# Order of steps and the scheduler's seed in a two-layer encoder trunk on one core

## The chip, the cores and the metric

The kernel runs on one core of a Trainium2 chip. The metric is the device time of one execution in microseconds (us). Before the change the median of three runs is 1641.14 us (1639.19 to 1641.91).

The names of the engines are those of the profile: PE is the tensor engine (matmuls; PEld are its weight loads), DVE the vector engine, ACT the scalar engine, POOL is GpSimd and SP the engine that only starts transfers (DMAs).

## The reference

Two layers, each a token sublayer and a channel sublayer, on x of 512 tokens by 1024 channels in float32:

```python
for i in range(DEPTH):
    proj = x @ w_in[i]
    q_na, k_na, v_na, q_r, k_r, v_r, g_r, gate_a, gate_b = jnp.split(proj, IN_SPLITS, axis=-1)
    ya = neighbourhood_attention(...)          # 8 heads of 64, windows of 8 rows x 16 columns
    yb = bidirectional_retention(q_r, k_r, v_r, g_r, ...)  # 4 heads, chunks of 128, rotary
    merged = sigmoid(gate_a) * (ya @ w_branch_a[i]) + sigmoid(gate_b) * (yb @ w_branch_b[i])
    x = layer_norm(ALPHA * x + merged @ w_out[i], ln1_g[i], ln1_b[i])
    ffn = conv_glu_ffn(x, w_up[i], conv_w[i], conv_b[i], w_down[i])     # width 2816, conv of 3 tokens
    ple = sigmoid(x @ w_ple_gate[i]) * (p[i] @ w_ple_proj[i])
    x = layer_norm(ALPHA * x + ffn + ple, ln2_g[i], ln2_b[i])
```

In `bidirectional_retention` q and k are rotated by position, scores between the tokens of a chunk are weighted with a decay, and a state of decayed k times v is carried from chunk to chunk, in both directions.

## The kernel before

**One matmul.** Every float32 operand is split in two: `hi` is its cast to a shorter format (ACT) and `lo` what is left (DVE subtracts). `mm3` (line 1181) makes three matmuls of each product, hi by hi, hi by lo and lo by hi. So each weight tile of 128x1024 (512 KB) comes in by a DMA (tiles `raw`, `rawa`, `rawt`), ACT writes `hi`, DVE writes `lo`, and only then PE can use it. In PE's rows, `u<-sx,lo` writes the accumulator `u` from the operands `sx` and `lo`.

**Seven products in place of eight.** Large products are cut into 2x2 blocks and done with seven products of sums of blocks, called a, c, t1, t2, d, t3, t4. The sums of weights are made in the loading: POOL adds a second weight tile to the first with an accumulating DMA, or, where two tiles are "mates", DVE adds them. The sums of x are made by `vg_sums` (line 1454), a generator that does one of its four steps each time it is called. In a step name the digit is the block, so `0t3` is product t3 of block 0.

**Stages of a layer.** First the v and g stretch (products of blocks 0 and 1, `vg`, line 1491; in layer 2 the gate block 9 too), then the fill stretch: q, k and gate blocks 2 to 8, the retention heads R0 to R3 and the neighbourhood heads N0 to N7. A retention head (`ret_head`, line 1625) takes several turns: PE transposes the rotated k (`kf`) to `kz`, DVE scales `kz`, PE makes scores `s` from `qk`, DVE weights them (`ta`, `a`, with the decay table `wx`), PE makes the state `st` from `kz` and v, DVE copies it to `su`, and PE writes the output `o` from `a`, `su` and `qx`. Then the output projection, the norm (`xn`, transposed by PE as `tr`), the gate of the layer embedding together with the first MLP segment (`pg`), and the other two MLP segments (`up_part`, `down`). `affine` (the steps A0 to A3) is six half-row DVE operations (two multiplications and four additions) that nothing on PE waits for soon; "g" is a plain tile of the up-projection without the seven products.

**What sets the order.** Every instruction is first recorded (`Program`, line 239) and emitted later by `run` (line 272), so all rows of the profile carry line 278. PE keeps the order in which the code asks for the matmuls, except that in the fill stretch it may choose among the next 10 groups (`FILL_WIN`). That order is written in tables: `VG` (v and g), `FILL`, `PG` (embedding gate and first MLP segment), `UP_ORDER` (segments 2 and 3), and `SUMS_AT` (at which steps of the v and g stretch a step of `vg_sums` is taken). ACT, DVE, POOL and SP are ordered by a list scheduler: `_dues` (line 422) gives each instruction a due time from the PE instructions that need it, `_order` (line 563) plays the whole program with modelled durations and picks the ready instruction with the earliest due, and `_best` (line 494) repeats that for 120 rounds with randomly raised due times, and keeps the round with the shortest modelled end. `SEED` starts the random numbers. There are two plans, one for each layer, from early in the v and g stretch to the end of the MLP. What lies outside keeps the order of the code.

**Mates.** `up_items` (line 931) makes the weight tiles of an MLP segment s; its last argument says whether t2 and t3 of a block take DVE's addition (mates) or POOL's.

Of the kernel before, what the change touches and what calls it, by code (L numbers as in the profile page):

```python
# [42 lines left out]
FILL_WIN = 10  # L43
FILL_AT = (36, 40, 56, 24, 28, 8, 20, 52)
FILL = (tuple('2a 7a 2c 7c 7t1 2t1 2t2 7t2 2d 7d 2t3 7t3 7t4 2t4 3a 8a R0 8c R1 3c R0 3t1 8t1 R1 R0 R1 8t2 R0 8d 8t3 3t2 3d 8t4 3t3 4a R1 4c 3t4 5a R2 4t1 5c R2 R3 R3 5t1 4t2 R2 5t2 R3 R2 4d 5d 5t3 4t3 R3 6a 6c 6t1 N0 N1 6t2 5t4 vn 6d N3 N1 6t3 4t4 6t4 vn N0 bb0 N2 vn vn bb2 N2 N0 N5 N2 N1 N3 N4 N6 bb3 bb1 N4 N5 N6 N6 bb4 N7 bb5 N4 N5 xn N3 N7 bb6 N7 bb7'.split()),
        tuple('9t2 X0 2a X1 2c X3 X2 9t3 9d 7a 7c 2t1 9t4 7t1 7t2 7d 2t2 2d 2t3 7t3 2t4 7t4 3a 8a R0 R0 3c 8c 3t1 R1 8t1 R1 R0 R1 8t2 R0 8d 8t3 3t2 3d 4a 8t4 3t3 R1 4c 3t4 5a R2 4t1 5c R2 R3 R3 5t1 4t2 R2 5t2 R3 R2 5d 5t3 4d 4t3 R3 6a 6c 6t1 N0 N1 6t2 5t4 vn 6d N3 N1 6t3 4t4 N0 vn 6t4 vn N2 N3 vn bb0 bb2 N0 N2 N5 N1 N2 N6 N4 N6 bb3 N4 bb1 N7 N5 N6 bb4 N4 bb5 bb7 N3 xn N5 N7 bb6 N7'.split()))
ORD = ('vector', 'scalar', 'tensor', 'gpsimd', 'sync')
BA = (tuple('0 1 2 3 4 5 6 7'.split()),
        tuple('0 1 2 3 4 5 6 7'.split()))
NORM = 'vector'  # L50
MATES = (1, 2)
FILL_MATES = ((), (0, 1))
WO = ('a', 'c', 't1', 't2', 'd', 't3', 't4a', 'T0', 't4b')

VG0 = ('p0', 'p1', '0a', '0c', '1a', '1c', 'ga0', '0t1', 'ga2', 'ga1', '0t2', '0d', '0t3', '1t1', '0t4', 'ga3', '1t2', '1d', '1t3', '1t4')
VG1 = ('0a', '0c', '1a', '1c', '9a', '0t1', '9c', '0t2', '0d', '1t1', '0t3', '0t4', '9t1', '1t2', '1d', '1t3', '1t4')
VG = (VG0, VG1)
SENT = ((20, 24), (24, 32))
CAST = ((32, 36), (44, 52))

TABLES_AT = ('0t4', '1t4')

PG = (tuple('a 0a T2 c S g S 0c S S g 1a t1 t2 0t1 1c 0t2 0d 0t3 1t1 0t4 d g 1t2 1d 1t3 t3 1t4 g t4'.split()),
        tuple('a 0a T2 S c S 0c 1a g g S 1c t1 0t1 S 0t2 t2 0d 0t3 1t1 0t4 1t2 1d 1t3 d 1t4 g t3 g t4'.split()))
PG_EARLY = "a"
A_DEEP = (4, 5, 5)
BOUND = ("p0", "t4a", "tr", "t4b", "p1")
VG_DEEP = 3
VG_PLAN = ("ga2", "0a")
SUMS_AT = (('1c', '0t1', 'ga1', 'ga2'), ('1c', '9a', '0t1', '9c'))  # L70
VG_EARLY = "d"
S_SEQ = ("t1", "d", "t2", "t3")
UP_ORDER = ((tuple('0a 0t1 A0 0c g A2 0t2 A3 A1 0d 0t3 1a 0t4 1t1 1c 1t2 1d 1t3 2a 1t4 2t1 2c 2t2 2d 2t3 s 2t4 s s'.split()), tuple('0a 0t1 0c g 0t2 0d 0t3 1a 0t4 1t1 1c 1t2 1d 1t3 2a 2t1 2t2 2d 2t3 2c 1t4 s 2t4 s s'.split())),
            (tuple('0a 0t1 A0 0c A1 g A2 0t2 A3 0d 0t3 1a 0t4 1t1 1c 1t2 1d 1t3 2a 1t4 2t1 2c 2t2 2d 2t3 s 2t4 s s'.split()), tuple('g 0a 0t1 0c g 0t2 0d 0t3 g 0t4 1a 1t1 1c 1t2 1d 1t3 s g s 1t4 s s'.split())))

DOWN = ("a", "c", "t1", "t2", "d", "t3", "t4")
# [8 lines left out]
SET = {1: dict(soon=5, hold=6, reserve=10, load=16, work=25, scale=1.0, spare=2, near=10, seed=0, shake=0.0), 2: dict(soon=5, hold=6, reserve=10, load=16, work=25, scale=1.0, spare=2, near=10, seed=0, shake=0.0)}  # L85
ROUNDS = 120
WALK = 12
SEED = 1


VG_HELD = (('0t1', '1t1', '0t2', '0c', '1t2', '1a', '1d', '1t3'), ('0a', '0c', '0t1', '1t1', '1t3', '1t2', '0t3', '0t2', '1d'))
# [7 lines left out]
def _up_order(l, s):  # L99

    return UP_ORDER[l][s - 1] if s else PG[l]


def _up_blocks(l, s):

    t0 = 2 * sum(SEGS[:s])
    return [t0 + 2 * b for b in range(sum(k[0].isdigit() and k.endswith("t4") for k in _up_order(l, s)))]
# [386 lines left out]
def _best(jobs, rounds=None):  # L494

    import random
    rnd = random.Random(SEED)
    rounds = rounds or ROUNDS
# [289 lines left out]
def trunk(tc, wpack, x_nat, x_tr, head, p_tr, rpb, decay, ln_par, ln_col, conv, cos_t, sin_t, dist, xi_d, zd, ident_d, out):  # L788
# [5 lines left out]
    with ExitStack() as es:  # L794
# [66 lines left out]
        def block_items(pos, held, early, n=2, mates=False):  # L861

            out = []
            prev = {}
            for kind, src, plus in (("a", "a", None), ("c", "c", None), ("t1", None, "b"), ("t2", None, "d"),
                                    ("d", "d", None), ("t3", "b", "d"), ("t4", None, "c")):
                for j in range(n):
                    at = lambda q: None if q is None else pos[q, j]
                    it = Item(kind, at(src), pos["a", j][3], plus=at(plus), own=kind in ("a", "t3"), pool=held.get(kind))
                    if kind in ("a", "t1", "t2", "t4"):  # L870
                        if j in prev:
                            prev[j].nxt = it
                        prev[j] = it
                    if kind == "t3":
                        [o for o in out if o.kind == early][j].early = it
                    out.append(it)
            if mates:
                t2, d, t3 = ([o for o in out if o.kind == k] for k in ("t2", "d", "t3"))
                for j in range(n):
                    t2[j].mate, t3[j].mate, d[j].then = d[j], d[j], t3[j]  # L880
            return out
# [49 lines left out]
        def up_items(l, s):  # L931

            t0, by = 2 * sum(SEGS[:s]), {}
            for b, t in enumerate(_up_blocks(l, s)):
                pos = {(q, 0): (l, UP0 + 2 * t + i, 0, 1024) for i, q in enumerate("acbd")}
                for it in block_items(pos, {}, VG_EARLY, 1, s in MATES):
                    by[f"{b}{it.kind}"] = [it]
            if s == 0:
                pos = {(q, j): (l, 74 + 2 * i + j, 0, 1024) for i, q in enumerate("acbd") for j in range(2)}
                for it in block_items(pos, {}, PG_EARLY):  # L940
                    by.setdefault(it.kind, []).append(it)
            out, c = [], UP0 + 2 * (t0 + 2 * len(_up_blocks(l, s)))
            for k in _up_order(l, s):
                if k in "gs":
                    out.append(Item(k, (l, c, 0, 1024), 1024))
                    c += 1
                elif k[0] not in "STA":
                    out += by[k]
            return out
# [369 lines left out]
        for i in range(2):  # L1319
            c = slice(i * 512, (i + 1) * 512)  # L1320
# [26 lines left out]
        def tables():  # L1347
            for t, d in ((cos_sb, cos_t), (sin_sb, sin_t), (xi_sb, xi_d.to_broadcast([P, 512])), (dist_sb, dist), (ident, ident_d)):
                nc.sync.dma_start(t, d)
            yield  # L1350
            for i in range(DEPTH):
                cws.append(bp.tile([P, 2 * NF, 4], F32, tag="cw", name=nm("cw")))
                nc.sync.dma_start(cws[i], conv[i])
            yield
# [69 lines left out]
        def ple_keep(l):  # L1424
            for t in range(4):
                nc.sync.dma_start(rscr[l][t * P:(t + 1) * P, :], pk[t])
            yield
# [7 lines left out]
        for l in range(DEPTH):  # L1435
# [265 lines left out]
            qn, kn, kl, vn = {}, {}, {}, {}  # L1701
# [117 lines left out]
            xn, xgb = [], []  # L1819
# [136 lines left out]
            if l == 0:  # L1956
                rest, first = second_half(), first_half()
                steps = {"p1": [first], "0a": [first], "1a": [ple_keep(l)], "0c": [rest], "1c": [rest], "0d": [rest], "0t3": [rest], "1t1": [rest]}
                for k in SUMS_AT[l]:
                    steps.setdefault(k, []).insert(0, sums)  # L1960
                steps.setdefault(SUMS_AT[l][3], []).append(rest)
                tab = tables()
# [207 lines left out]
            N1, N2 = slice(0, 512), slice(512, 1024)  # L2170
# [160 lines left out]
            def pg():  # L2331
# [95 lines left out]
            for s in (len(SEGS) - 1,):  # L2427
# [180 lines left out]
                t4 = products("t4", x4, s == 0)  # L2608
# [160 lines left out]
```

## Time and profile before

| | |
|---|---|
| median of the runs | 1641.14 us (1639.19 to 1641.91) |
| the profiled execution | 1638.68 us |
| its span | 1636.9 us, so 1.8 us lie outside it |
| granted clock of PE | 0.999 of full |
| busy in the span | PE 1622.0, DVE 1388.8, ACT 1025.7, POOL 251.8 us |
| moved by DMA | 360.57 MB, mean 220 GB/s |

In a row of the timeline stand the start, the duration, the engine, the operation, the output and the inputs, and in brackets how long the engine had stood idle before and what ended it. Matmuls overlap: a row's duration is longer than the distance to the next row's start, and that distance is what a matmul costs. A row with "x2" holds two instructions that ran without a gap. A row "PE w <- DVE lo: 1.1, 2, 0.7" of the waits says that PE stood 1.1 us in two waits for DVE's lo before matmuls into w, 0.7 at most in one.

### The profile page before, as it was taken

Reading aid. Unit: us, or ns where it says so; the run is one execution under the profiler, and the core shown is the slowest. Engines: PE = TensorE matmul, PEld = TensorE weight load, DVE = VectorE, ACT = ScalarE, POOL = GpSimd, SP = SyncE. Lnnn points to the kernel's source line nnn. Section 1 sums busy time; section 2 is a strip of 40 time slices with the busy share of each in tenths; the row PEclk is TensorE's granted clock in tenths of the full one; section 3 lists DMA queues with packets and bytes.
Section 4 is the critical chain, followed back from the end, with each engine's and each line's share of the span. In section 5 each row is a group of like instructions: output and inputs, shape, how many; then the busy total and the mean of one; then the engine's idle time right before and its main releaser. Section 6 shows DMA issues by size and latency. Waiting matters only on the chain.

```text
span 1636.9 us, 26381 instructions
## 1 busy us (share of the span) xinstructions
PE 1622.0 (99%) x10005; PEld 1460.9 (89%) x10005; DVE 1388.8 (85%) x2122; ACT 1025.7 (63%) x1545; POOL 251.8 (15%) x296
## 2 busy tenths in 40 slices
PE   9999999999999999999999999999999999999997
PEld 7889999888889899899888999998888898998986
DVE  6757998778978999879998779986799799997798
ACT  6665768645567657556486457785456676673564
POOL 1210211101210112002111112210012111110113
PEclk9999999999999999999999999999999999999999
DMA  9996677859798879768688868788598988778675
GB/s 310 274 240 153 164 162 199 278 189 291 176 307 213 234 226 220 239 195 221 185 253 213 256 162 200 172 221 259 195 260 214 296 237 244 223 185 271 166 178 129
DMA packets 108032, 360.57 MB, mean 220 GB/s; under 512 B 12800, under 2 KB 14336, under 8 KB 107904
## 3 DMA queue, kind: packets, MB, share of 16 engines
q0 software_dynamic: 36432, 130.56, 40.5%
q1 hardware_dynamic: 71472, 228.31, 38.6%
q8 instruction: 79, 1.29, 0.3%
q14 instruction: 49, 0.40, 0.1%
HBM read 327.37 MB, written 27.79 MB: 217 GB/s over the span
## 4 chain that ended last, share of the span: by engine, by line
PE 81%; DVE 10%; issue 4%; DMA 3%; POOL 1%; ACT 1%; DVEq 0%; POOLq 0%; ACTq 0%
PE u L278 31%; PE v L278 15%; PE gt L278 15%; PE w L278 7%; PE gn L278 4%; DVE lo L278 4%; PE o L278 2%; DMA rawa<-in_wpack 2%; DVE xn L278 1%; PE x L278 1%; PE ns L278 1%; PE na L278 1%; DVE ga L278 1%; PE pt L278 1%; DMA raw<-in_wpack 1%
## 5 line engine op out<-in xcount | busy, mean ns | idle before, releaser
L278 DVE TENSOR_TENSOR lo<-rawa,hi 128x1024 fp32r<-128x1024 f32 (+1 forms) x230 | 274.6, 1199 | 50.2 <-ACT hi L278 39.9
L278 ACT CAST hi<-rawa 128x1024 fp32r<-128x1024 f32 (+1 forms) x230 | 236.0, 1035 | 122.9 <-DMA rawa<-in_wpack 70.1
L278 POOL DMA_DIRECT2D rawa<-in_wpack x159 | 141.0, 899 | 1035.1 <-DVE lo L278 775.8
L278 DVE TENSOR_TENSOR lo<-raw,hi 128x1024 fp32r<-128x1024 f32 (+1 forms) x170 | 203.8, 1204 | 17.7 <-ACT hi L278 17.6
L278 ACT CAST hi<-raw 128x1024 fp32r<-128x1024 f32 (+1 forms) x146 | 150.7, 1039 | 20.1 <-PE u L278 10.2
L278 PE MATMUL gt<-x1t,hi 128*128 128x512 f32 x448 | 138.6, 390 | 0.2 <-DVE x1t L278 0.2
L278 PEld LDWEIGHTS gt<-x1t,hi 128*128 128x128 f32 x448 | 83.0, 188 | 16.9 <-DVE x1t L278 0.6
L278 PE MATMUL u<-xt,hi 128*128 128x256 f32 x480 | 87.4, 283 | 0.0
L278 PE MATMUL u<-x1t,hi 128*128 128x256 f32 x480 | 87.3, 283 | 0.0
L278 PE MATMUL gt<-x1t,lo 128*128 128x512 f32 x224 | 87.2, 390 | 0.0
L278 PE MATMUL v<-sh,hi 128*128 128x256 f32 x304 | 86.3, 284 | 0.5 <-ACT uh L278 0.5
L278 PE MATMUL u<-sh,hi 128*128 128x256 f32 x304 | 86.5, 284 | 0.0
L278 PE MATMUL v<-sh,lo 128*128 128x256 f32 x304 | 86.2, 283 | 0.0
L278 PE MATMUL v<-sl,hi 128*128 128x256 f32 x304 | 86.0, 283 | 0.0
L278 PE MATMUL u<-sh,lo 128*128 128x256 f32 x304 | 86.0, 283 | 0.0
L278 PE MATMUL u<-sl,hi 128*128 128x256 f32 x304 | 86.0, 283 | 0.0
L278 PE MATMUL v<-lo,sh 128*128 128x512 f32 x216 | 84.1, 389 | 0.0
L278 PE MATMUL v<-hi,sh 128*128 128x512 f32 x216 | 84.1, 389 | 0.0
L278 PE MATMUL v<-hi,sl 128*128 128x512 f32 x216 | 84.0, 389 | 0.0
L278 PE MATMUL gt<-ybt,hi 128*128 128x512 f32 x256 | 79.5, 392 | 0.0
L278 PE MATMUL u<-lo,sh 128*128 128x512 f32 x200 | 78.0, 390 | 0.1
L278 PE MATMUL u<-hi,sh 128*128 128x512 f32 x200 | 77.9, 389 | 0.0
(311 smaller groups left out, 4935.5 us busy)
## 6 DMA issues: line engine op xcount, KB each, us to landing
raw<-in_wpack SPq DMA_DIRECT2D x166, 512.0 KB, 6.8
rawa<-in_wpack POOLq DMA_DIRECT2D x153, 512.0 KB, 7.0
rawa<-in_wpack SPq DMA_DIRECT2D x56, 512.0 KB, 6.6
rawt<-in_wpack SPq DMA_DIRECT2D x56, 512.0 KB, 6.1
rawt<-in_wpack POOLq DMA_DIRECT2D x41, 512.0 KB, 9.1
hi<-in_wpack POOLq DMA_DIRECT2D x37, 512.0 KB, 6.7
sx<-s_scr SPq DMA_DIRECT2D x32, 512.0 KB, 9.5
lo<-in_wpack POOLq DMA_DIRECT2D x13, 512.0 KB, 8.2
```

Source lines behind the costliest of these rows:

```text
L278: r = o.call(*[real(x) for x in o.a], **{k: real(v) for k, v in o.k.items()})
```

## The change

Seven entries change. The steps of the PE tables move, one condition is written in another way, and the seed is another one. Of the long FILL table only the piece that changes is shown, and of UP_ORDER the piece of layer 1, segment 2.

```diff
 FILL[1]:
-  ... 2t4 7t4 3a 8a R0 R0 3c 8c 3t1 R1 ...
+  ... 2t4 7t4 3a 8a 3c R0 R0 8c 3t1 R1 ...
-MATES = (1, 2)
+MATES = (((), (0, 1, 2), (0, 1, 2)), ((), (0, 1, 2), (0, 1, 2)))
-VG1 = ('0a', '0c', '1a', '1c', '9a', '0t1', '9c', '0t2', '0d', '1t1', '0t3', '0t4', '9t1', '1t2', '1d', '1t3', '1t4')
+VG1 = ('0a', '0c', '1a', '1c', '9a', '0t1', '9c', '0t2', '0d', '1t1', '0t3', '1t2', '1d', '1t3', '1t4', '0t4', '9t1')
 PG[0]:
-  a 0a T2 c S g S 0c S S g 1a t1 t2 0t1 1c 0t2 0d 0t3 1t1 0t4 d g ...
+  a 0a T2 c S g 0c S S g S 1a t1 t2 0t1 0t2 0d 0t3 1t1 0t4 1c d g ...
-SUMS_AT = (('1c', '0t1', 'ga1', 'ga2'), ('1c', '9a', '0t1', '9c'))
+SUMS_AT = (('1c', '0t1', 'ga1', 'ga2'), ('1c', '9a', '0t1', '0t1'))
 UP_ORDER[0][0]:
-  0a 0t1 A0 0c g A2 0t2 A3 A1 0d 0t3 1a ...
+  0a 0t1 g A0 0c A2 0t2 A1 0d 0t3 A3 1a ...
-SEED = 1
+SEED = 7
...
-                for it in block_items(pos, {}, VG_EARLY, 1, s in MATES):
+                for it in block_items(pos, {}, VG_EARLY, 1, b in MATES[l][s]):
```

The instructions are the same ones before and after on every engine. What differs is their order, in both plans, and three places show how.

The first is DVE in the second MLP segment of layer 1, before the `lo` of `rawt_1029`, the weight sum of step 0t3. The `xn` rows are those of the steps A1 and A3, with the norm's scale and offset `lnh`; `uh` is a half of an up tile, `gg` its gated form and `R` the residual. Before:

```order
L278 TENSOR_TENSOR rawt_1029_6073<-rawt_1029_6073,raw_6037 128x1024
L278 TENSOR_TENSOR lo_6280<-rawa_6054,hi_6195 128x1024
L278 TENSOR_TENSOR xn_4459<-xn_4459,lnh_5961 128x512
L278 TENSOR_TENSOR xn_4459<-xn_4459,lnh_5965 128x512
L278 TENSOR_TENSOR xn_4368<-xn_4368,lnh_5965 128x512
L278 TENSOR_TENSOR lo_6314<-raw_6037,hi_6128 128x1024
L278 TENSOR_TENSOR xn_4459<-xn_4459,lnh_5968 128x512
L278 TENSOR_TENSOR xn_4459<-xn_4459,lnh_5975 128x512
L278 TENSOR_TENSOR xn_4368<-xn_4368,lnh_5968 128x512
L278 TENSOR_TENSOR xn_4368<-xn_4368,lnh_5975 128x512
L278 TENSOR_TENSOR uh_6204<-uh_6204,w_6215 128x2x256
L278 TENSOR_TENSOR lo_6352<-rawt_1029_6073,hi_6282 128x1024
```

And after:

```order
L278 TENSOR_TENSOR rawt_1029_6068<-rawt_1029_6068,raw_6056 128x1024
L278 TENSOR_TENSOR lo_6313<-raw_6056,hi_6204 128x1024
L278 SCALAR_TENSOR_TENSOR gg_6282<-gt_6207,cw_4866,gg_6282 128x511
L278 TENSOR_TENSOR R_4952<-R_4952,xn_4412 128x512
L278 SCALAR_TENSOR_TENSOR gg_6282<-gt_6207,cw_4866,gg_6282 128x511
L278 TENSOR_TENSOR lo_6351<-rawt_1029_6068,hi_6315 128x1024
```

Between the sum and its lo stood ten rows, seven of them of A1 and A3; now four stand there, and one is of an affine step.

The second is ACT in the fill stretch of layer 2, around the copy of `v` to `uh`, the first half of q/k block 2 (`rawt_1559` and `rawt_1562` are weight sums t3). Before:

```order
L278 CAST hi_9791<-rawa_9256 128x1024
L278 CAST hi_9795<-raw_9695 128x1024
L278 ACTIVATE sgb_9824<-u_8959 128x512
L278 CAST hi_9829<-raw_9731 128x1024
L278 ACTIVATE uh_9855<-v_9797 128x2x256
L278 CAST hi_9883<-rawa_9479 128x1024
L278 COPY u_1553_9885<-u_9531 128x512
L278 CAST hi_9914<-rawt_1559_9667 128x1024
```

And after:

```order
L278 CAST hi_9789<-rawa_9280 128x1024
L278 CAST hi_9792<-raw_9696 128x1024
L278 ACTIVATE sgb_9823<-u_8958 128x512
L278 CAST hi_9827<-rawt_1559_9626 128x1024
L278 ACTIVATE uh_9855<-v_9796 128x2x256
L278 CAST hi_9859<-rawa_9302 128x1024
L278 COPY u_1553_9887<-u_9494 128x512
L278 CAST hi_9890<-rawt_1562_9628 128x1024
```

The cast just ahead of `uh` was that of a plain weight `raw`; now it is that of `rawt_1559`, which came three rows behind `uh` before.

The third is DVE at the first retention head of layer 1. `qk_1634` (before) and `qk_1633` (after) are the same `lo` part of the rotated k, an operand of the scores. Before:

```order
L278 TENSOR_TENSOR ta_1636<-s_1578,wx_1393 128x512
L278 TENSOR_TENSOR qk_1634<-kf_1492,qk_1634 128x512
L278 TENSOR_TENSOR lo_1642<-raw_1433,hi_1539 128x1024
L278 TENSOR_TENSOR ta_1649<-s_1588,wx_1393 128x512
L278 SCALAR_TENSOR_TENSOR kz_1632<-kz_1599,zeta,kz_1632 128x128 x3
L278 TENSOR_TENSOR qk_1651<-t_226_1574,qk_1651 128x512
```

And after:

```order
L278 TENSOR_SCALAR wx_1596<-dist_sb,nlg 128x384
L278 TENSOR_TENSOR qk_1594<-t_226_1573,qk_1594 128x512
L278 SCALAR_TENSOR_TENSOR wx_1596<-dist_sb,lgs,wx_1596 128x384
L278 TENSOR_TENSOR lo_1631<-raw_1432,hi_1537 128x1024
L278 TENSOR_TENSOR qk_1633<-kf_1496,qk_1633 128x512
L278 TENSOR_TENSOR ta_1642<-s_1576,wx_1596 128x512
```

The lo of the next weight has gone from behind this qk to ahead of it, and the `lo` part of the rotated q (from `t_226`) from behind both to ahead of both.

More of the change, by code (lines that the diff above doesn't have):

```diff
@@ L45 @@
 FILL = (tuple('2a 7a 2c 7c 7t1 2t1 2t2 7t2 2d 7d 2t3 7t3 7t4 2t4 3a 8a R0 8c R1 3c R0 3t1 8t1 R1 R0 R1 8t2 R0 8d 8t3 3t2 3d 8t4 3t3 4a R1 4c 3t4 5a R2 4t1 5c R2 R3 R3 5t1 4t2 R2 5t2 R3 R2 4d 5d 5t3 4t3 R3 6a 6c 6t1 N0 N1 6t2 5t4 vn 6d N3 N1 6t3 4t4 6t4 vn N0 bb0 N2 vn vn bb2 N2 N0 N5 N2 N1 N3 N4 N6 bb3 bb1 N4 N5 N6 N6 bb4 N7 bb5 N4 N5 xn N3 N7 bb6 N7 bb7'.split()),
-        tuple('9t2 X0 2a X1 2c X3 X2 9t3 9d 7a 7c 2t1 9t4 7t1 7t2 7d 2t2 2d 2t3 7t3 2t4 7t4 3a 8a R0 R0 3c 8c 3t1 R1 8t1 R1 R0 R1 8t2 R0 8d 8t3 3t2 3d 4a 8t4 3t3 R1 4c 3t4 5a R2 4t1 5c R2 R3 R3 5t1 4t2 R2 5t2 R3 R2 5d 5t3 4d 4t3 R3 6a 6c 6t1 N0 N1 6t2 5t4 vn 6d N3 N1 6t3 4t4 N0 vn 6t4 vn N2 N3 vn bb0 bb2 N0 N2 N5 N1 N2 N6 N4 N6 bb3 N4 bb1 N7 N5 N6 bb4 N4 bb5 bb7 N3 xn N5 N7 bb6 N7'.split()))
+        tuple('9t2 X0 2a X1 2c X3 X2 9t3 9d 7a 7c 2t1 9t4 7t1 7t2 7d 2t2 2d 2t3 7t3 2t4 7t4 3a 8a 3c R0 R0 8c 3t1 R1 8t1 R1 R0 R1 8t2 R0 8d 8t3 3t2 3d 4a 8t4 3t3 R1 4c 3t4 5a R2 4t1 5c R2 R3 R3 5t1 4t2 R2 5t2 R3 R2 5d 5t3 4d 4t3 R3 6a 6c 6t1 N0 N1 6t2 5t4 vn 6d N3 N1 6t3 4t4 N0 vn 6t4 vn N2 N3 vn bb0 bb2 N0 N2 N5 N1 N2 N6 N4 N6 bb3 N4 bb1 N7 N5 N6 bb4 N4 bb5 bb7 N3 xn N5 N7 bb6 N7'.split()))
 ORD = ('vector', 'scalar', 'tensor', 'gpsimd', 'sync')
@@ L61 @@
 TABLES_AT = ('0t4', '1t4')
-PG = (tuple('a 0a T2 c S g S 0c S S g 1a t1 t2 0t1 1c 0t2 0d 0t3 1t1 0t4 d g 1t2 1d 1t3 t3 1t4 g t4'.split()),
+PG = (tuple('a 0a T2 c S g 0c S S g S 1a t1 t2 0t1 0t2 0d 0t3 1t1 0t4 1c d g 1t2 1d 1t3 t3 1t4 g t4'.split()),
         tuple('a 0a T2 S c S 0c 1a g g S 1c t1 0t1 S 0t2 t2 0d 0t3 1t1 0t4 1t2 1d 1t3 d 1t4 g t3 g t4'.split()))
@@ L69 @@
 VG_PLAN = ("ga2", "0a")
-SUMS_AT = (('1c', '0t1', 'ga1', 'ga2'), ('1c', '9a', '0t1', '9c'))
+SUMS_AT = (('1c', '0t1', 'ga1', 'ga2'), ('1c', '9a', '0t1', '0t1'))
 VG_EARLY = "d"
 S_SEQ = ("t1", "d", "t2", "t3")
-UP_ORDER = ((tuple('0a 0t1 A0 0c g A2 0t2 A3 A1 0d 0t3 1a 0t4 1t1 1c 1t2 1d 1t3 2a 1t4 2t1 2c 2t2 2d 2t3 s 2t4 s s'.split()), tuple('0a 0t1 0c g 0t2 0d 0t3 1a 0t4 1t1 1c 1t2 1d 1t3 2a 2t1 2t2 2d 2t3 2c 1t4 s 2t4 s s'.split())),
+UP_ORDER = ((tuple('0a 0t1 g A0 0c A2 0t2 A1 0d 0t3 A3 1a 0t4 1t1 1c 1t2 1d 1t3 2a 1t4 2t1 2c 2t2 2d 2t3 s 2t4 s s'.split()), tuple('0a 0t1 0c g 0t2 0d 0t3 1a 0t4 1t1 1c 1t2 1d 1t3 2a 2t1 2t2 2d 2t3 2c 1t4 s 2t4 s s'.split())),
             (tuple('0a 0t1 A0 0c A1 g A2 0t2 A3 0d 0t3 1a 0t4 1t1 1c 1t2 1d 1t3 2a 1t4 2t1 2c 2t2 2d 2t3 s 2t4 s s'.split()), tuple('g 0a 0t1 0c g 0t2 0d 0t3 g 0t4 1a 1t1 1c 1t2 1d 1t3 s g s 1t4 s s'.split())))
```

## The prediction

> **What bounds the kernel now.** I read the page first, then the waits of the tensor engine (PE), then the timeline around each wait. The page gives the span and shares:
>
> ```profile
> span 1636.9 us, 26381 instructions
> PE 1622.0 (99%) x10005; PEld 1460.9 (89%) x10005; DVE 1388.8 (85%) x2122; ACT 1025.7 (63%) x1545; POOL 251.8 (15%) x296
> PE 81%; DVE 10%; issue 4%; DMA 3%; POOL 1%; ACT 1%; DVEq 0%; POOLq 0%; ACTq 0%
> ```
>
> PE is busy for 99% of the span. The change reorders the same instructions, so its matmuls cost the same, and only the time in which PE stands can change. The waits of PE name it (total, times, longest):
>
> ```profile
> PE warm L278 <- DVE warm L278: 1.2, 1, 1.2
> PE w L278 <- DVE lo L278: 1.1, 2, 0.7
> PE st L278 <- DVE kz L278: 1.1, 2, 0.7
> PE u L278 <- DVE lo L278: 1.0, 1, 1.0
> PE tr L278 <- DVE xn L278: 0.5, 2, 0.3
> PE v L278 <- ACT uh L278: 0.5, 1, 0.5
> PE u L278 <- DVE ve L278: 0.4, 1, 0.4
> PE o L278 <- DVE qx L278: 0.2, 1, 0.2
> PE gt L278 <- DVE x1t L278: 0.2, 1, 0.2
> ```
>
> Without the first, a start-up wait that the change does not reach, that is 5.0 us in 11 waits. A wait costs more than its idle time. The timeline of PE at one of them, and at one of 512 columns:
>
> ```profile
> 946.36 0.28 PE L278 MATMUL u<-sh,lo 128*128 128x256 f32 x1
> 947.11 0.39 PE L278 MATMUL v<-sh,hi 128*128 128x256 f32 x1 [0.47 <-ACT uh L278]
> 947.33 0.28 PE L278 MATMUL v<-sl,hi 128*128 128x256 f32 x1
> 947.45 0.28 PE L278 MATMUL v<-sh,lo 128*128 128x256 f32 x1
> ...
> 458.46 0.39 PE L278 MATMUL gt<-x1t,lo 128*128 128x512 f32 x1
> 458.69 0.39 PE L278 MATMUL gt<-x1t,hi 128*128 128x512 f32 x1
> 459.25 0.50 PE L278 MATMUL gt<-x1t,hi 128*128 128x512 f32 x1 [0.17 <-DVE x1t L278]
> ```
>
> Undisturbed, 128x256 matmuls start 0.12 us apart and 128x512 ones 0.23. The one at 947.11 would have started at 946.48: 0.63 lost, and the next start comes 0.22 instead of 0.12 later, 0.10 more. So 0.47 of idle cost 0.73, and I price each wait at its idle time plus 0.26. The eleven then cost 5.0 + 11 x 0.26 = 7.9 us, 0.5% of the span. That is the most that order can give in the middle; a wait that has no tag, at 862.94 below, adds a little.
>
> **The change part by part.** The table for the mates is rewritten with equal effect: segments 1 and 2 have blocks 0 to 2 at most, all of them are listed, and segment 0 has none in either form. It costs 0. The rest moves instructions of ACT, DVE, POOL, SP and PE inside the two planned stretches. On each engine the multiset of instructions is the same, so I go from wait to wait and count, in the order of after, what now stands ahead of what PE waited for.
>
> *First retention heads of layer 1.* DVE, then PE:
>
> ```profile
> 164.79 0.68 DVE L278 TENSOR_TENSOR qk<-kf,qk 128x512 fp32r<-128x512 f32 x1
> 165.38 1.22 DVE L278 TENSOR_TENSOR lo<-raw,hi 128x1024 fp32r<-128x1024 f32 x1
> 165.14 0.60 PE L278 MATMUL kz<-ident,kf 128*128 128x128 f32 x4
> 166.66 0.39 PE L278 MATMUL w<-xt,lo 128*128 128x256 f32 x1 [0.68 <-DVE lo L278]
> 179.15 0.50 PE L278 MATMUL st<-vh,kz 128*128 128x256 f32 x2 [0.73 <-DVE kz L278]
> ```
>
> Before, PE does kz, then w, then the scores s; after, s comes first, at the place of kz (165.14). The lo of w now stands ahead of the second qk that s reads. A row of 1024 columns takes DVE 1.14 us (457.37 to 458.51 below), so qk is done at 164.79 + 0.68 + 1.14 = 166.61, and s waits 1.47 + 0.10, say 1.6. The waits at 166.66 (0.68 + 0.26 = 0.94) and 179.15 (0.73 + 0.26 = 0.99) go: lo has the time of kz and s to spare, and the wx, ta, t and p steps that stood ahead of kz have moved behind it. **-0.3.**
>
> *The transposed x1 for a plain up tile g in layer 1's first MLP segment.* DVE before the wait at 459.25 above:
>
> ```profile
> 457.37 1.22 DVE L278 TENSOR_TENSOR lo<-raw,hi 128x1024 fp32r<-128x1024 f32 x1
> 458.51 0.68 DVE L278 TENSOR_TENSOR x1t<-xf,x1t 128x512 fp32r<-128x512 f32 x1
> ```
>
> After, this lo and two 512-column rows (0.60 each, 592.36 to 592.96 below) no longer stand ahead of x1t, and one such row newly does: 1.14 + 1.20 - 0.60 = 1.74 earlier, for 0.17 of idle. **-0.43.**
>
> *MLP segment 2 of layer 1, product 0t3 (UP_ORDER).*
>
> ```profile
> 571.83 1.22 DVE L278 TENSOR_TENSOR lo<-rawa,hi 128x1024 fp32r<-128x1024 f32 x1 [1.73 <-ACT hi L278]
> 592.36 0.68 DVE L278 TENSOR_TENSOR uh<-uh,w 128x512 f32<-128x512 f32 x1
> 592.96 1.22 DVE L278 TENSOR_TENSOR lo<-rawt,hi 128x1024 fp32r<-128x1024 f32 x1
> 594.23 0.39 PE L278 MATMUL u<-sx,lo 128*128 128x256 f32 x1 [1.00 <-DVE lo L278]
> ```
>
> From 571.83 to this lo DVE has no idle time. With A3, six half-rows, moved behind 0t3 and A0 moved after g, the order of after has 0.47 us less ahead of this lo, and 2.99 us of the work between moves ahead of the idle 1.73 at 571.83 and fills it. The lo ends near 592.96 + 1.22 - 0.47 - 1.73 = 591.98; PE wants it at 594.23 - 1.16 = 593.07. **-1.26**, with 1.1 to spare; A3 then waits on nothing of PE's.
>
> *Layer 2, v and g stretch.*
>
> ```profile
> 861.67 1.22 DVE L278 TENSOR_TENSOR lo<-rawa,hi 128x1024 fp32r<-128x1024 f32 x1
> 862.41 0.39 PE L278 MATMUL u<-hi,sh 128*128 128x512 f32 x1
> 862.94 0.50 PE L278 MATMUL u<-lo,sh 128*128 128x512 f32 x1
> ```
>
> The step of 0.53 against 0.23 has no tag, but starts as lo ends (862.89). Another lo and a 1024-column mate sum, 2.28 us, no longer stand ahead of it. **-0.30.**
>
> *The copy of v in layer 2's first q/k block* (the wait at 947.11). ACT, then the totals of 920 to 960 (PE, PEld, DVE, ACT, POOL, clock, DMA share, GB/s):
>
> ```profile
> 945.51 1.05 ACT L278 CAST hi<-raw 128x1024 fp32r<-128x1024 f32 x1 [3.99 <-DMA raw<-in_wpack]
> 920.00:960.00 40.00, 39.53 (x328) 39.19 (x327) 22.80 (x25) 21.92 (x28) 6.57 (x8) 1.00 0.94 240
> ```
>
> DVE is half idle here; ACT stood 3.99 us in a cast for which a weight had not landed, and the copy uh that PE needs was queued behind it. After, the cast ahead of uh is of another weight (a t3), whose load moves from SP's row 296 to 293 and past two writes of gate scratch. I take it to land in time: **-0.73.** If the cover is gone, 0.73 stays. By this row the 16 DMA engines are 0.94 busy, so an earlier issue is not surely an earlier landing; hence 0.7 for the term, and a rival below.
>
> The Trainium skill, page "DMA: Bandwidth & Descriptors", section "Issuing engines are not separate DMA queues", says that copies started by SP, ACT or GpSimd all run on the same 16 DMA engines and interleave; by it the lead at the queue would be shared out, and the sum below would be -1.8 instead of -2.6. The trace's share of 0.94 agrees with it and does not decide it.
>
> *First retention heads of layer 2* (the second w and st waits, 0.4 each of the totals above, and o 0.2: 1.0 + 3 x 0.26 = 1.8). 3c moves ahead of both R0, and PE now takes 3a after the product 2t4, not before it. lo of w is early now, but kz stands behind three lo and six small rows and su behind two statistics: by my count DVE gives st about 1.0 too late and o about 0.7. **0**, between -1.8 (all three go) and +1.0 (all as late as the largest wait of this kind, 0.73 + 0.26, thrice).
>
> *Transposes of layer 2's first norm.*
>
> ```profile
> 1262.66 0.80 DVE L278 TENSOR_SCALAR xn<-xn,mv,rstd 128x1024 f32<-128x1024 f32 x1
> 1263.52 0.66 PE L278 MATMUL tr<-ident,xn 128*128 128x128 f32 x4 [0.34 <-DVE xn L278]
> ```
>
> One lo (1.14) no longer stands ahead of xn. 0.34 + 0.26: **-0.60.** The other tr wait and the one on ve keep their order and stay.
>
> *New waits.* At three places more DVE work stands ahead than before, by up to 1.2 us where I count 1.0 of slack: +0.35 together. What the order does not show (landings, ACT table work) I price below by 0 and above by three mean waits, 3 x 7.9 / 11 = 2.2, since a reshuffled order of the same kind may stop PE in places as the old one does; I take one mean wait, +0.72, as most of after's order is as far ahead of PE as before's.
>
> **Sum:** -0.3 - 0.43 - 1.26 - 0.30 - 0.73 - 0.60 + 0.35 + 0.72 = -2.55. The profiled execution took 1638.68 (its span and 1.8 around it), 2.46 below the median. 1638.68 - 2.55 = 1636.13, and at the median's ratio, 1641.14 / 1638.68, **1638.6**. Changes under 0.2% (3.3 us) can hardly be told from none here.
>
> **Rivals.** *Faster by more:* nothing unforeseen comes (-0.72) and the layer 2 heads lose their three waits (-1.8): -5.1, so 1636.0. For it: DVE has 22.80 of 40 us of work ahead of these heads, and can be early. Against: kz is moved behind three lo.
>
> *Nothing to tell:* weights bound 947, and the 0.73 stays because bandwidth, not the issue, sets the landing; the heads of layer 2 pay their +1.0. -2.55 + 1.73 = -0.8: 1640.3. For it: 0.94 DMA share. Against: one weight only, moved past two writes. The rule of the Trainium skill named above is this rival's first half.
>
> *Slower:* the accumulated weight of layer 2's product 2t4 lands late. DVE's lo of it, PE's product, and these transfers from 920 to 960:
>
> ```profile
> 962.15 1.23 DVE L278 TENSOR_TENSOR lo<-rawa,hi 128x1024 fp32r<-128x1024 f32 x1 [1.40 <-ACT hi L278]
> 967.56 0.40 PE L278 MATMUL u<-xt,hi 128*128 128x256 f32 x2
> rawa<-in_wpack POOLq DMA_DIRECT2D x6, 512.0 KB, 8.5
> ```
>
> After, 24 matmuls of 3a no longer precede this product: it comes 2.88 earlier, at 964.68, and its first lo at 964.92, against 963.38: 1.5 of slack. Beyond that DVE's rotation for R0 hangs on it, and each us is PE's. If POOL issues the sum one such transfer later (8.5, the median here, last row), PE loses 7.0: -2.55 + 7.0 = +4.4, 1645.6. It turns the sign from 4.1 us of delay. For it: its two accumulates stand one and two rows later in POOL's queue. Against: POOL is busy for 15%, and 1.5 us of slack covers a small delay.
>
> **Numbers.** Forecast 0.45, faster by more 0.20, nothing to tell 0.25, slower 0.10. Around the forecast I allow 1.2 us either way for the terms taken from bounds, so 0.13 of its 0.45 passes -3.3; with 0.19 of the second and 0.03 of the others faster is 0.35. Slower is 0.07 of the last and 0.01 of the rest, 0.08; the same 0.57. The range leaves out a tenth on either side: from 1635.0, an us below the faster rival, to 1642.5, 2.2 above the null.
>
> **What would show it.** Right: the waits at 459, 594, 862, 947 and 1263 gone, PE waiting for qk (not kz) near 166, total PE idle some 2 us less. Wrong: ACT again in a cast before uh at 947; a long wait of PE for lo near 965; waits of over 1 us at new places, above all with DVE busy without a break before them.

## The result and the profile after

| | before | after |
|---|---|---|
| median of 16 runs each | 1639.8 us (1638.54 to 1642.97) | 1637.14 us (1636.3 to 1638.4) |
| ratio, 95% interval | | 0.9981 (0.9973 to 0.9989) |
| span of the profiled execution | 1636.9 us | 1635.4 us |

The changed kernel takes 0.19% less, some 3.1 us (1.8 to 4.4): the ratio is that of the means, and the medians differ by 2.7. The forecast was 2.55 us, 0.16%. The page of after shows no less work on PE; DVE has 1.6 us more busy time, and the kernel still ends earlier:

```profile
span 1635.4 us, 26401 instructions
PE 1622.0 (99%) x10005; PEld 1460.9 (89%) x10005; DVE 1390.4 (85%) x2122; ACT 1027.0 (63%) x1545; POOL 246.3 (15%) x296
```

The waits of PE in after (total, times, longest), without the start-up wait, which is 1.2 us as before:

```profile
PE u L278 <- DVE ve L278: 1.1, 1, 1.1
PE s L278 <- ACT qk L278: 0.5, 1, 0.5
PE u L278 <- DVE uh L278: 0.4, 1, 0.4
PE o L278 <- DVE qx L278: 0.4, 1, 0.4
PE s L278 <- DVE qk L278: 0.3, 1, 0.3
PE v L278 <- DVE lo L278: 0.3, 1, 0.3
PE u L278 <- DVE x1t L278: 0.2, 1, 0.2
PE tr L278 <- DVE xn L278: 0.2, 1, 0.2
```

That is 3.4 us in 8 waits instead of 5.0 in 11. The waits for lo of w, kz, lo of the weight sum, uh on ACT and the x1t of a gt tile are gone; s, uh on DVE, a lo of v and another x1t are new, and the one on ve is more than twice as long. At the price of the prediction (idle time plus 0.26) the tagged waits cost 3.4 + 8 x 0.26 = 5.5 us instead of 7.9, which is 2.4 less.

The two spans differ by only 1.5 us. The profiled execution of before was 1.1 us faster than the median (1638.68 against 1639.8), that of after lay at its median (1637.16), and it also started late: its first retention scores begin at 161.29 us, in the kernel with layer 1 alone changed, whose order up to there is the same, at 160.61. Of these 0.7 us, 0.6 lie in the first eight matmuls into `gn`, which take 2.87 us in one execution (5.08 to 7.95) and 2.25 in the other (5.01 to 7.26). So 0.7 us lie between two executions of one order. Single spans can't settle a change of this size; the timed rounds and the places of the waits do.

### The profile page after: what moved, and what is told of

The parts are those of the page before. It is cut to its first block, busy times and chain, and to the rows that moved or that the text cites. A ratio compares the mean times of both kernels' runs of the same rounds, so it can differ in the third digit from the quotient of the medians.

```text
span 1635.4 us, 26401 instructions
## 1 busy us (share of the span) xinstructions
PE 1622.0 (99%) x10005; PEld 1460.9 (89%) x10005; DVE 1390.4 (85%) x2122; ACT 1027.0 (63%) x1545; POOL 246.3 (15%) x296
## 4 chain that ended last, share of the span: by engine, by line
PE 84%; DVE 11%; issue 2%; DMA 2%; POOL 1%; ACT 0%; DVEq 0%; POOLq 0%; ACTq 0%
PE u L278 31%; PE v L278 17%; PE gt L278 15%; PE w L278 8%; PE gn L278 4%; DVE lo L278 3%; PE o L278 2%; DMA rawa<-in_wpack 2%; DVE xn L278 1%; PE x L278 1%; PE ns L278 1%; PE na L278 1%; DVE t L278 1%; PE pt L278 1%; DVE ga L278 1%
## 5 line engine op out<-in xcount | busy, mean ns | idle before, releaser
L278 ACT ACTIVATE uh<-u 128x512 f32<-128x512 f32 x69 | 41.1, 596 | 63.1 <-PE u L278 62.9
```

The costliest lines, as they stand in the source:

```text
L278: r = o.call(*[real(x) for x in o.a], **{k: real(v) for k, v in o.k.items()})
```

## The experiments

An edit of a table makes the search order everything anew, so a part of the change cannot be undone alone by editing. Where an experiment moves rows, the order that the search found for ACT, DVE, PE, POOL and SP was written down, and the kernel replays it with the named rows moved. All were timed in five rounds beside the kernel before.

| kernel | ratio to before, 95% | us against before |
|---|---|---|
| the change | 0.9981 (0.9973 to 0.9989) | -3.1 |
| layer 1 alone | 0.9992 (0.9983 to 1.0001) | -1.3 |
| layer 2 alone | 0.9993 (0.9984 to 1.0002) | -1.1 |
| before, three rows moved | 0.9988 (0.9979 to 0.9997) | -2.0 |
| the same, four affine rows later | 0.9982 (0.9973 to 0.9992) | -3.0 |
| before, 19 rows moved | 0.9978 (0.9970 to 0.9987) | -3.6 |
| after, rows moved at seven places | 0.9980 (0.9972 to 0.9989) | -3.3 |
| after, rows moved and ten affine rows a layer later | 1.0044 (1.0031 to 1.0057) | +7.2 |
| seed 7 alone | 1.0006 (0.9997 to 1.0015) | +1.0 |
| tables alone | 0.9988 (0.9980 to 0.9997) | -2.0 |
| tables alone, rows moved at four places | 0.9991 (0.9982 to 1.0000) | -1.5 |
| after, four affine rows back | 1.0000 (0.9991 to 1.0009) | 0.0 |

The last column is (ratio - 1) x 1640. Intervals are about 1.5 us wide on either side, so differences under that are read from the waits.

### One layer at a time

```diff
-the order that the search found for both layers, with the tables of both
+layer 1 alone: tables and order of after in layer 1, of before in layer 2
+layer 2 alone: tables and order of before in layer 1, of after in layer 2
```

> The changed kernel's tables and its order of every instruction in layer 1, the old ones in layer 2. Theory (places): what PE loses at a place is set by the few rows that stand ahead there on DVE or ACT, so the change is a sum of places and the layers are independent. By the two profiles the order of layer 1 is worth -1.5 us: the waits at 459 and 594 us go, the heads near 166 us lose 1.3 instead of 2.2, and the wait near 435 us costs 1.3 instead of 0.7; layer 2 shows its old waits at their old length. About 1638.3 where before takes 1639.8. Rival (flow): DVE's backlog only moves, so part of this is lost again in layer 2's order, which was searched together with the old layer 1: -0.5 or less.

> The old tables and order in layer 1, the changed ones in layer 2. Places: -1.0 us: the waits at 862 and 947 us go and the retention heads near 990 us lose 1.0 us less, but new waits near 1255, 1397, 1400 and 1410 us cost 2.3. Together with the kernel that has only layer 1's part it adds up to the whole change, -2.5. Flow: no such sum, above 0 or below -2.

Measured: -1.3 and -1.1 us, which add up to -2.4 of the -3.1. Of PE's waits, those that tell the layers apart, in the kernel with layer 1 alone and then in that with layer 2 alone:

```profile
PE u L278 <- DVE ve L278: 1.3, 1, 1.3
PE v L278 <- ACT uh L278: 0.6, 1, 0.6
```

```profile
PE u L278 <- DVE lo L278: 1.7, 3, 1.0
PE u L278 <- DVE ve L278: 0.4, 1, 0.4
```

Each layer has the waits of the kernel whose order it took: the first keeps the old wait on uh (layer 2) and has the longer one on ve (layer 1); in the second the old lo wait of layer 1 is there (1.0 of the 1.7) and that on uh is gone. Nothing here speaks against independent layers and the sum fits, but each part alone is within reach of zero, so the times don't show it.

### Three rows, and then the queue

```diff
 DVE, layer 1, MLP segment 2
+lo (of rawt, step 0t3)
 xn (A3) x2
 xn (A1) x2
 uh
-lo (of rawt, step 0t3)
 ACT, layer 2, q/k block 2
+uh<-v
 CAST hi<-raw
-uh<-v
 DVE, layer 2, first norm
+xn<-xn,mv,rstd
 lo
-xn<-xn,mv,rstd
```

> The kernel before, its order untouched but for three rows: the lo of layer 1's weight sum t3 stands ahead of four affine rows (590 us), the copy of v to uh ahead of a cast whose weight is late (946 us), the normalise of xn ahead of a lo (1262 us). Places: the waits at 594, 947 and 1263 us go whole, 1.4 + 0.9 + 0.6 = -2.9 us, as much as the whole change brings, without another seed or another step. Flow: the rows that are passed are late next, and at most half of it, -1.4, stays.

Measured: -2.0. The waits at 947 and 1263 us are gone whole, though the one on the lo of w near 980 us grew from 0.46 to 0.82. The one at 594 is gone too, but at 600 us there is one of the same length. PE, then DVE of this kernel:

```profile
600.03 0.47 PE L278 MATMUL u<-x1t,hi 128*128 128x256 f32 x2 [1.04 <-DVE uh L278]
590.20 1.22 DVE L278 TENSOR_TENSOR lo<-rawt,hi 128x1024 fp32r<-128x1024 f32 x1
599.19 0.69 DVE L278 TENSOR_TENSOR uh<-uh,u 128x512 f32<-128x512 f32 x1
```

lo ends at 591.42 instead of 594.18, and the addition into uh, behind the same rows as before, ends at 599.88: PE reaches the next operand earlier and waits there for 1.04 + 0.26 us. Here moving a row within a full DVE queue only chose at which operand PE pays. Both theories had a part of it: places at 947 and 1263, where the passed row is late for nobody, flow at 594.

How full DVE is, the totals of after show (window, PE, PEld, DVE, ACT, POOL):

```profile
580.00:600.00 20.00, 19.89 (x148) 18.93 (x147) 20.00 (x28) 10.14 (x12) 1.73 (x2) 1.00 0.78 259
600.00:620.00 20.00, 20.00 (x169) 20.00 (x168) 20.00 (x24) 14.37 (x19) 4.26 (x6) 1.00 0.83 208
```

DVE is busy for 19.76 or more of each 20 us from 580 to 680, and for 11.83 of the 20 after that. The expectation below takes it to be full from 560 on. It is not: in the kernel with three rows it stands 0.40 us at 568 and 1.27 at 572, both times for a `hi` of ACT.

The next kernel takes work out of the piece of the queue ahead of 600 us:

```diff
 (three rows moved as above), DVE, layer 1, MLP segment 2
-xn (A3) x2
 ...
-R<-R,xn (A3) x2
 ...
 uh<-uh,u
 lo
 uh<-uh,v
+xn (A3) x2
+R<-R,xn (A3) x2
```

> The kernel with three rows moved had lost its wait at 594 us and had a new one at 600 us of the same length (PE waits there for DVE to add u and v into uh). Here four affine rows of A3 (4 x 0.60 = 2.4 us) stand behind those additions too. New theory (queue): DVE has no idle time from 560 to 660 us, so a row moved there within the same piece of its queue moves the wait on; only work taken out of the piece ends it. By it the wait at 600 goes and none takes its place, -1.3 us against the kernel with three rows, -3 against before. Rival (places, as in the prediction): what is late is the few rows nearest to the wait, and the four rows are late at the next place: the same time as with three rows.

Measured: -3.0, as expected by the queue. In its profile the addition into uh ends at 596.95, and PE passes 599 us without a gap (DVE, then PE):

```profile
596.27 0.68 DVE L278 TENSOR_TENSOR uh<-uh,u 128x512 f32<-128x512 f32 x1
599.05 0.40 PE L278 MATMUL u<-x1t,hi 128*128 128x256 f32 x2
599.29 0.28 PE L278 MATMUL u<-x1t,lo 128*128 128x256 f32 x1
```

Seven rows moved by hand take off as much as the whole change. They do it in another way, though: in after A3's rows still stand ahead of this addition (see the part on MLP segment 2 in the section on the prediction).

### The same edit undone in after

```diff
 DVE, layer 1, MLP segment 2
+xn (A3) x4
 lo (of rawt, step 0t3)
-xn (A3) x2
 uh
-xn (A3) x2
```

> The changed kernel with four affine rows of A3 (2.4 us of DVE) put back ahead of the lo of step 0t3's weight sum, all else as it is. In its profile this lo ends at 593.02 and PE takes it at 593.31, so it has 0.3 us to spare: a wait of 2.1 comes up there, and the wait of 0.3 near 599 us goes: +1.9 us against the changed kernel, -0.6 against before. If the place of A3 does not matter (the seed's other rows bring the change), 0 against the changed kernel, -2.5 against before.

Measured: 0.0 against before, so +3.1 against the change, where 1.9 was expected. PE and DVE, then the totals of the 4 us behind the wait (PE, PEld, DVE, ACT, POOL, granted clock of PE, DMA share, GB/s):

```profile
595.30 0.39 PE L278 MATMUL u<-sx,lo 128*128 128x256 f32 x1 [2.09 <-DVE lo L278]
594.03 1.22 DVE L278 TENSOR_TENSOR lo<-rawt,hi 128x1024 fp32r<-128x1024 f32 x1
595.30:599.30 4.00, 4.00 (x21) 4.00 (x21) 2.89 (x4) 0.29 (x1) 0.00 (x0) 0.57 0.02 6
```

The wait is as long as foretold. What was not foretold stands behind it: for these 4 us the granted clock is 0.57, where it is 1.00 up to the wait, and the 128x256 matmuls start 0.21 us apart instead of 0.12. That costs another 1.5 us, so the price of idle time plus 0.26 falls short for this wait. With it the expected 1.9 becomes 3.4, within the interval. The wait on ve is longer too, 1.6 us here and 1.1 in after, with its rows untouched; in the kernel with layer 1 alone it is 1.3, so it differs between executions of one order. The four rows' place decides whether PE waits at 594 us; the 3.1 us is not the gain of that place alone, as a part of it is the slower clock.

### Seed and tables

```diff
-SEED = 1
+SEED = 7
```

(on the kernel before: seed 7 alone; the reverse on the changed kernel: tables alone)

> The kernel before with seed 7 and none of the tables. If the seed carries the change, -2.5 us and the waits at 459, 862, 947 and 1263 us gone. If the tables do, 0. Queue and places alike: a searched order is not made of parts, so other waits of the same size come; between -2.5 and +2 us, and the sum with the tables alone is not the whole.

> The changed tables with seed 1. If the tables carry the change, -2.5 us; if the seed does, 0. Queue: A3 behind 0t3 takes 3.6 us of DVE work out of the piece before 600 us whatever the seed, so the waits at 594 and 600 us are gone here too, and missing work in other places decides the rest: between -2.5 and +1 us.

Measured: +1.0 for the seed, -2.0 for the tables. The longest wait of PE with seed 7 alone:

```profile
PE v L278 <- ACT uh L278: 2.4, 1, 2.4
```

The wait on uh is five times that of before. On ACT, in that kernel:

```profile
949.54 1.04 ACT L278 CAST hi<-raw 128x1024 fp32r<-128x1024 f32 x1 [5.90 <-DMA raw<-in_wpack]
950.49 0.59 ACT L278 ACTIVATE uh<-v 128x512 f32<-128x512 f32 x1
```

It is the same pair of rows as in before, with a landing 4 us later; the row ahead of them starts 2.1 us later too. The tables alone have none of the lo waits near 594 and no uh wait at 600 or 947:

```profile
PE u L278 <- DVE ve L278: 1.3, 1, 1.3
PE s L278 <- DVE qk L278: 0.6, 2, 0.3
PE o L278 <- DVE su L278: 0.6, 1, 0.6
PE w L278 <- ACT xf L278: 0.5, 1, 0.5
```

So the tables carry -2.0 of the -3.1, and the 1.1 that the seed adds to them is within the intervals. Seed 7 gives no better order by itself: with the old tables it makes other waits, some of them longer. The reason given for the tables does not hold: in this kernel, as in after, A3's rows stand ahead of the addition into uh (597.57 us), and not behind it.

### Moving all that waits

```diff
 after, at seven places: the row that PE waits for
+xn<-xn,u (434), qk (166), qx (990), x1t (1254), lo (1397), lo (1400), uh x2 (1409)
 the DVE or ACT rows that stood ahead of it
-xn<-xn,u (434), qk (166), qx (990), x1t (1254), lo (1397), lo (1400), uh x2 (1409)
```

> The changed kernel, with the rows moved ahead that PE waits for in its own profile: the addition into xn ahead of a lo (434 us), the two halves of the rotated k ahead of the decay table (166 us), qx ahead of two ta rows (990 us), x1t ahead of a lo and of statistics (1254 us), two lo ahead of affine rows and of another lo (1397, 1400 us), two uh ahead of a gg row (1409 us). Places: these waits cost 1.3 + 1.3 + 0.7 + 0.8 + 1.5 = 5.6 us, and -4.5 to -5.5 of them come out against the changed kernel, -7 to -8 against before (1632 to 1633). Flow: half or less, -2.5 against the changed kernel.

Measured: -3.3 against before, so no gain over the change that can be told, where places wanted -5. By its profile PE's waits are 2.6 us in 8, which at the same price is 0.8 less than in after. Two of the new ones:

```profile
589.23 0.38 PE L278 MATMUL v<-sx,lo 128*128 128x256 f32 x1 [0.29 <-DVE lo L278]
995.28 0.50 PE L278 MATMUL o<-su,qx 128*128 128x256 f32 x2 [0.65 <-DVE su L278]
```

The first stands in the full stretch, where after had none: what PE won ahead of it, it gave back in part there. The second is qx's neighbour: qx went ahead, and su is late in its place.

> The changed kernel with rows moved ahead as in the first try (without qx, which made su late), and with ten affine rows in each layer (6 us of DVE work) moved behind the first block of the MLP segment. Queue: the waits near 589, 598, 1402 and 1409 us that stood after the first try, 0.5 each, go; with what that try won, -2.0 to -3.0 us against the changed kernel, -4.5 to -5.5 against before (about 1635). Rival: the affine rows make the operands of the segment's end late, and the time is that of the first try, 0 to -0.5 against the changed kernel.

```diff
 (after, moved as above without qx), DVE
-xn and R rows of A1 and A3 (layer 1), of A2 and A3 (layer 2), ten rows each, from ahead of the second block
+the same ten rows behind the lo rows of the second block
```

Measured: +7.2. The lazy rows were put together in one place, ahead of the next block's uh (PE twice, then DVE ahead of the first wait):

```profile
622.14 0.73 PE L278 MATMUL u<-x1t,hi 128*128 128x256 f32 x2 [4.76 <-DVE uh L278]
1437.40 0.47 PE L278 MATMUL u<-x1t,hi 128*128 128x256 f32 x2 [4.46 <-DVE uh L278]
593.07 1.23 DVE L278 TENSOR_TENSOR lo<-rawa,hi 128x1024 fp32r<-128x1024 f32 x1 [2.88 <-ACT hi L278]
```

Ten rows are 6.0 us of DVE; PE waited 4.8 and 4.5 behind them, and here too the granted clock behind the waits is low, 0.54 from 622 to 624 us. Both the queue theory's number and its rival's were wrong here. Two things had not been counted: what the next operand behind the new place could bear, and that DVE, without the lazy rows, stood 2.88 us at 593 (2.91 in layer 2) for a `hi` of ACT, a time that these rows had filled in after.

> The kernel before with the seven rows moved as in the last but one try (three ahead, four affine rows of A3 behind 600 us) and twelve more: the addition into xn ahead of a lo (434), one s3 row behind x1t (459), lo ahead of a ta and a qk row (166), the eight kz rows ahead of decay and ta rows (178), a lo behind another lo (862). Queue: in these stretches DVE has idle time soon after, so the passed rows are late for nobody: the waits cost 0.7 + 0.4 + 1.0 + 0.7 + 0.4 = 3.2 us, two thirds of it or more come out, -5 to -6 against before. Rival: what is passed is late next, as with the first three rows in the MLP: -3, no more than the seven rows alone.

```diff
 (seven rows moved as above), DVE and ACT
+xn<-xn,u ahead of lo (434); x1t ahead of s3 (459); lo ahead of ta, qk (166); kz x8 ahead of wx, t, ta (178); lo<-rawa ahead of lo<-raw (862)
```

Measured: -3.6, where -5 to -6 was expected. The waits on ve, x1t and the lo near 862 are gone, but the heads of layer 1 wait for a and su instead, and sl near 667 us is new (PE):

```profile
180.02 0.51 PE L278 MATMUL o<-vh,a 128*128 128x256 f32 x2 [0.51 <-DVE a L278]
181.22 0.50 PE L278 MATMUL o<-su,qx 128*128 128x256 f32 x2 [0.34 <-DVE su L278]
666.65 0.50 PE L278 MATMUL v<-hi,sl 128*128 128x512 f32 x1 [0.34 <-DVE sl L278]
```

> The changed tables with seed 1, and six pieces moved: both rotated operands and a lo ahead of a ta row (166), su ahead of a lo (185), the addition into xn ahead of a lo (434), qk ahead of decay rows and of the other qk on ACT and on DVE (987). Queue: the waits of its profile there cost 1.3 + 0.8 + 1.5 + 0.6 = 4.2 us; two thirds or more come out: -3 against the tables alone, -4.5 to -5.5 against before. Rival: -2 against before, as the tables alone.

```diff
 (tables alone), DVE and ACT
+qk x2 and lo ahead of ta (166); su ahead of lo (185); xn<-xn,u ahead of lo (434); qk ahead of wx, qk (987)
```

Measured: -1.5, where -4.5 to -5.5 was expected; the rival was nearer. PE's waits at the two head places, where I had meant to end them:

```profile
168.19 0.47 PE L278 MATMUL s<-qk,qk 128*128 128x256 f32 x2 [0.97 <-DVE ta L278]
990.29 0.38 PE L278 MATMUL st<-vh,kz 128*128 128x256 f32 x1 [0.67 <-DVE kz L278]
```

ta, which I passed, holds the accumulator that the second scores need, and kz is late once qk goes first. At the first of the two, DVE is busy for 4.99 of the 5 us from 165 to 170, and the passed row is the next operand. At the second it is not full, 8.31 of the 10 us from 980 to 990: there DVE itself had stood 0.43 us for ACT's part of kz. No version here beats the change by more than its interval; the best, before with 19 rows moved, is at 0.9978 against 0.9981.

## Why the prediction was right, and where its steps were not

The forecast of -2.55 us came true in sign and size (-3.1, 1.8 to 4.4). The five old waits that it named went, most of them for the reason that it gave. That the sum came out is luck in part: a gain that it put at nothing (the heads of layer 2, about -1.2) and new waits that it put at half their size balanced. With the terms as the traces have them, the sum would be -2.0; the other 1.1 us of the measured 3.1 are not assigned to any place, and lie within the interval.

**Right.** The waits at 459, 594, 862, 947 and 1263 us are gone, as the list of signs had it, and PE waits for qk near 166. The table for the mates changes nothing that shows. 24 matmuls no longer precede 2t4's product, but the slower rival's wait near 965 is absent.

**First retention heads of layer 1: -0.3.** After, PE waits twice in s:

```profile
166.67 0.50 PE L278 MATMUL s<-qk,qk 128*128 128x256 f32 x2 [0.47 <-ACT qk L278]
167.48 0.39 PE L278 MATMUL s<-qk,qk 128*128 128x256 f32 x1 [0.31 <-DVE qk L278]
```

0.73 and 0.57 make 1.3 instead of the 1.6 that I had; the old waits of 1.93 are gone, so -0.6. I had one wait, for DVE; the first half of it is ACT's, which writes the cast part of qk. PE keeps next to nothing of this gain: it waits it away on ve (below).

**MLP segment 2: -1.26, with 1.1 to spare.** The wait went, but lo had 0.3 to spare (after, DVE, PE, DVE, DVE):

```profile
591.80 1.21 DVE L278 TENSOR_TENSOR lo<-rawt,hi 128x1024 fp32r<-128x1024 f32 x1
593.31 0.28 PE L278 MATMUL u<-sx,lo 128*128 128x256 f32 x1
566.97 1.23 DVE L278 TENSOR_TENSOR lo<-rawa,hi 128x1024 fp32r<-128x1024 f32 x1 [0.35 <-ACT hi L278]
598.28 0.67 DVE L278 TENSOR_TENSOR uh<-uh,u 128x512 f32<-128x512 f32 x1
```

The mechanism was right. DVE's idle time of 1.73 us ahead of this lo is 0.35 now, and the rows ahead of it are the 0.47 us less that I had. The two profiles are best counted from PE's matmul behind ve (434.49 before, 435.18 after): this lo starts 156.62 us later, in before 158.47, so 1.85 sooner instead of my 2.20, as 0.35 of the idle time stayed. PE wants it 0.45 sooner, by the term for the gt tile, which I had not taken off the spare time. 1.1 - 0.35 - 0.45 = 0.3.

What the step lacked is the next operand, the addition into uh, for which PE waits when only lo is moved (the kernel with three rows). In after nothing was taken out ahead of this addition: 791 DVE rows precede it, of the same kinds as in before and with three rows, A3's among them. Counted from ve it starts 163.10 us later, with three rows 164.49, so 1.39 sooner, and 1.32 of that is idle time that DVE no longer has near 570 us (0.40 and 1.27 with three rows, 0.35 in after). PE comes 0.48 sooner, so most of the 1.04 us is gone. PE still stands there for 0.11 us (599.10), 0.37 with its price. So two ways lead past 600 us: taking rows out of the full piece, as the seven rows by hand do, or filling the idle time at its start, as the change does. The second is read from the rows and was not tried by itself.

**The copy of v: -0.73, with a chance of 0.7.** The wait is gone in after, and in the way that I took: the cast of the t3 weight ahead of uh starts with no idle time, so its weight had landed, and uh waits only for PE to finish v (ACT of after):

```profile
940.40 1.05 ACT L278 CAST hi<-rawt 128x1024 fp32r<-128x1024 f32 x1
942.79 0.60 ACT L278 ACTIVATE uh<-v 128x512 f32<-128x512 f32 x1 [1.34 <-PE v L278]
```

The landing was not needed, though. In the kernel with three rows (ACT) uh stands ahead of the cast; the weight still lands after it and PE does not wait:

```profile
944.04 0.60 ACT L278 ACTIVATE uh<-v 128x512 f32<-128x512 f32 x1 [2.28 <-PE v L278]
945.21 1.05 ACT L278 CAST hi<-raw 128x1024 fp32r<-128x1024 f32 x1 [0.57 <-DMA raw<-in_wpack]
```

So bandwidth, the first half of my "nothing to tell" rival, did not keep the 0.73: what decides is which row stands ahead of uh in ACT's queue, and whether its weight has landed. The Trainium skill, page "PSUM — Partial Sum Buffer", section "Engine vs sequencer instructions", states that the queues of ScalarE, VectorE and GpSimd are "strict FIFO"; the rows with seed 7 alone agree, where uh starts only after the cast that stood 5.90 us for its weight.

**First retention heads of layer 2: 0.** They lose less: after has one tagged wait there, 0.39 + 0.26 for qx at 991 us, instead of three of 1.8 together. The term was mis-sized by about 1.2 us. My count had st 1.0 late behind kz; no tagged wait on kz is left.

**New waits: +0.35 + 0.72.** They are the term that was most wrong. The wait on ve, which I held for unchanged since its own rows keep their order, grew from 0.41 to 1.09, and in layer 2 one came up in the first MLP segment and two in the second (PE of after):

```profile
435.18 0.47 PE L278 MATMUL u<-hi,mt 128*128 128x512 f32 x1 [1.09 <-DVE ve L278]
1255.30 0.73 PE L278 MATMUL u<-hi,x1t 128*128 128x512 f32 x2 [0.24 <-DVE x1t L278]
1400.84 0.39 PE L278 MATMUL v<-sx,lo 128*128 128x256 f32 x1 [0.27 <-DVE lo L278]
1409.92 0.47 PE L278 MATMUL u<-x1t,hi 128*128 128x256 f32 x2 [0.42 <-DVE uh L278]
```

At idle time plus 0.26 these are 0.68 (the growth) + 0.50 + 0.53 + 0.68 = 2.4 us, where I had 1.07. Two of the causes can be read from DVE (before; after; after):

```profile
383.93 1.23 DVE L278 TENSOR_TENSOR lo<-rawa,hi 128x1024 fp32r<-128x1024 f32 x1 [3.39 <-ACT hi L278]
384.63 1.22 DVE L278 TENSOR_TENSOR lo<-rawa,hi 128x1024 fp32r<-128x1024 f32 x1 [4.09 <-ACT hi L278]
1381.38 1.22 DVE L278 TENSOR_TENSOR lo<-rawa,hi 128x1024 fp32r<-128x1024 f32 x1 [1.02 <-ACT hi L278]
```

From the first of these rows DVE has no idle time up to the wait on ve, 50.56 us later in before; from the second it is 50.55 in after. ACT, which makes the `hi` of both, had stood 4.17 and 4.86 us for the weight to land. So the end of this wait hangs on a landing 50 us ahead, and what PE won in the heads only makes it wait longer: from the first scores to the matmul behind ve it takes 274.10 us in before and 273.89 in after.

The third row is the opposite of what happened at 572 us in layer 1: one row of 0.60 us fewer stands ahead of this lo, and DVE stands 1.02 us there for ACT's `hi`, where in before it has no idle time from 1360 to 1420 us. PE's waits at 1401 and 1410 follow. Like the idle time at 572, this is read from the rows and was not tried by itself.

Put into the prediction's sum, in its order and at its price: -0.6 - 0.43 - 1.26 + 0.37 (at 599) - 0.30 - 0.73 - 1.2 (heads of layer 2) - 0.60 + 2.4 + 0.34 (at 1397, 0.08 of idle without a tag) = -2.0.

## What to carry to other kernels

Before a row is moved ahead of a wait, take the totals of the engine that is waited for by short windows. Where it is full, moving a row ended one wait and made the next; what helped was work taken out of the full piece, or idle time of that engine at the start of the piece filled with rows that are needed later. Even where it had some room, the rows moved by hand in the heads won less than their waits had cost. Lazy work can fill such idle time: four rows put behind the tight operands cost nothing, ten at one place passed nearly whole to PE. To test a part of a searched order, write the order down and move rows in it: editing the table makes the search deal all cards anew.

## What the runs showed of the hardware that was not expected

A wait of 2.09 us was followed by 4 us at a granted clock of 0.57, and one of 4.76 us by 0.54 in the 2 us behind it, with 128x256 matmuls 0.21 us apart instead of 0.12. Behind one of 2.42 us (seed 7 alone, 951 to 953 us) the clock was 1.00, so these runs give no length from which on it happens. The same order of instructions started 0.7 us later in one execution than in another (first scores at 161.29 and 160.61), which is a quarter of the effect under study. And four rows of 2.4 us put ahead of an operand that had 0.3 us to spare made a wait of 2.09 us: nothing of DVE's delay was absorbed beyond that slack.
